# Moving a four-column transpose into an early matmul bank, and regrouping a chain of table transfers, in a two-layer fp32 decoder trunk

## The chip, the cores and the metric

One core of a Trainium2 chip runs the whole kernel in one launch. The metric is the device time of that core in microseconds (us). The kernel before was timed three times: median 1132.03 us, from 1131.14 to 1132.06 us. PE is the matmul engine (PEld its weight loads), ACT the scalar engine, DVE the vector engine, POOL the GpSimd engine; SP only issues transfers.

## The reference, cut to what matters

The input is one sequence of 512 tokens with 1024 features, all in fp32. Two layers are computed: attention and an MLP, then a short convolution mixer and a second MLP.

```python
for layer in range(2):
    if layer == 0:   # attention: 8 forgetting heads, 8 stick-breaking heads, width 64
        proj = rms_norm(h, attn_norm) @ attn_w_in
        q_fox = rms_norm(q[:, :8], fox_q_gain); k_fox = rms_norm(k[:, :8], fox_k_gain)
        q_sb  = rms_norm(q[:, 8:], sb_q_gain);  k_sb  = rms_norm(k[:, 8:], sb_k_gain)
        ...
        h = h + concat(o_fox, o_sb) @ attn_w_out
    else:            # short convolution
        b, c, u = split(rms_norm(h, conv_norm) @ conv_w_in)
        h = h + (b * causal_dwconv(c * u, conv_kernel)) @ conv_w_out
    u = causal_dwconv(rms_norm(h, ffn_norm[layer]) @ ffn_w_up[layer], ffn_conv[layer])
    h = h + (silu(u[:, :2816]) * u[:, 2816:]) @ ffn_w_down[layer]
```

Two things in it matter here. Each head's queries and keys are multiplied by a gain vector of 64 values (the head norms' factors). And the up-projection of each MLP multiplies 1024 features by a 1024 x 5632 matrix.

## The kernel before, in words

**Products.** Every fp32 operand is split into a high part (written by ACT, line 293 for weights) and a low part (DVE subtracts, line 294), and each product is three matmuls: high by high, high by low, low by high (lines 314 to 316, or 571 to 573 where tokens are the output rows). Weights come from DRAM through three `raw` buffers, issued by SP.

**The start.** The input `x_tok` arrives in four pieces. For each of eight blocks of 128 features, `take(f)` turns the block on PE (four transposes, line 857), ACT writes its high part (line 862) and DVE its low part (line 863). Between the blocks PE already runs the first head pair's key product, which is the first product of `queries_keys(0)`; the list `ORDER` says how many of its eight steps follow each block. Instructions of this stage are chained by `in_line`, which forces an instruction behind the last one that was chained on the same engine. After the eighth block come the rest of the key product, the whole query product, and then `values(0)`, the first value product: four token blocks of 24 matmuls (L571 to L573). PSUM is cut into banks by tag; tag `a` has two banks, `b` four and `c` two, each tag handed out in turn, and a bank must be read out before its next user may write.

The head gains (`heads_in`, four rows fetched by POOL at line 127) must be turned from rows into a column on every partition: one transpose (L188) into a `c` bank, a copy to `head_gains` (L189) and two scalings (L191). The kernel before asks for this step 4.0 us of counted PE work after the loads were issued (`after(HEADS, ...)`); it is then placed behind the query product. ACT's copy of each product out of its bank (L659) multiplies by `head_gains`, so it needs this step; and the first value product writes the `a` bank that the key product's copy frees. The sums of squares for the head norms (L608, eight small matmuls) and the transpose of the small parameters (L179) are placed behind it too.

**The up-projections.** Most of each MLP's up-projection, and the convolution's input projection, use Strassen-like forms on 2 x 2 blocks: seven block products (p1, p7, p3, p6, p2, q5, q4) instead of eight, class `Sevens`. A group of 256 output columns takes seven slots, one form each, 24 matmuls of about 0.12 us (L1055) a slot. The slot code also loads the next blocks (X, Y, W, Z on SP's queue, L1070, L1071, L1079) and adds blocks in flight (POOL, accumulating transfers, L1082). For the convolution the groups are 1 to 4, so there are 28 slots and three more behind them. Two X buffers exist; the group's p1 is made from X (ACT and DVE, L1003 and L1005), then Y gets X added (L1112), and only then may X be overwritten by an accumulating transfer, for q5.

**The tables.** For the MLPs the sums of blocks are made ahead in DRAM (`table_steps`): transfers of 256 rows x 768 columns, issued by POOL, alternately a copy (L104) and an accumulation (L101), each waiting for the one before it when it reads or changes the same table. The second MLP has 24 of them. The kernel takes steps from this generator by `sum_far(n)`: `FAR = 7, 1, 14` means seven after the attention, one at each of the convolution's slots 1, 8 and 15, and fourteen at slot 20. All POOL transfers go through one queue in program order.

Of the kernel before, what the change touches and what calls it, by code (L numbers as in the profile page):

```python
# [22 lines left out]
ALU = mybir.AluOpType  # L23
# [6 lines left out]
ND = D // P  # L30
DFF = 2816
NF = DFF // P
HD = 64
# [6 lines left out]
PRE = 12.0  # L40
SUM_STEP = 0.6
WARM = 34
HEADS, NORM0 = 4.0, 4.6
ORDER = (1, 0, 1, 1, 1, 1, 3)
SUMS, FLAT, ROWS = 3.0, 1.5, 8.0
NSUMS, NROWS, LATE = 4.0, 3.0, 7.0
FILL1, FILL2, BEFORE = 1.5, 3.3, 2.0
UNITS = (0, 1), (2,), (3,)
PLAIN = 2
FAR = 7, 1, 14  # L50
CHUNKS = (2, 3), (5, 3), (8, 3)
SHARE = 0.58

# [2 lines left out]
def trunk(  # L56
# [7 lines left out]
    act, dve, pe, pool = nc.scalar, nc.vector, nc.tensor, nc.gpsimd  # L64
# [12 lines left out]
    def bank(tag):  # L77
        n_ps[0] += 1
        return ps.tile([P, S], F32, tag=tag, name=f"ps{tag}{n_ps[0]}", bufs={"a": 2, "b": 4, "c": 2}[tag])
# [43 lines left out]
    heads_in = xin.tile([4, P], F32, tag="heads_in", name="heads_in")  # L123

    def load_heads():
        for i, g in enumerate((fox_q_gain, fox_k_gain, sb_q_gain, sb_k_gain)):
            nc.gpsimd.dma_start(heads_in[i:i + 1, :].rearrange("o (j d) -> o j d", j=2), g[:, None, :].to_broadcast([1, 2, HD]))
# [26 lines left out]
    ident = const.tile([P, P], F32, tag="ident", name="ident")  # L154
# [20 lines left out]
    head_gains = const.tile([P, 4], F32, tag="head_gains", name="head_gains")  # L175
# [7 lines left out]
            pe.transpose(t[:, i * 66:(i + 1) * 66], taps_in[:, i, :], ident[0:66, 0:66])  # L183
        dve.tensor_copy(taps, t[:, 0:4 * 66])

    def load_head_gains():
        t = bank("c")
        pe.transpose(t[:, 0:4], heads_in, ident[0:4, 0:4])  # L188
        dve.tensor_copy(head_gains, t[:, 0:4])  # L189
        for i in (0, 2):  # L190
            dve.tensor_scalar(head_gains[:, i:i + 1], head_gains[:, i:i + 1], HD ** -0.5, None, op0=ALU.mult)  # L191

    def gain_of(norm, f):
        return gains[:, norm + f:norm + f + 1]
# [9 lines left out]
    def behind(later, earlier):  # L204

        tc.add_manual_dep(
            later.ins, earlier.ins.name,
            mybir.DependencyInfo(mybir.DependencyClass.NoSync, mybir.DependencyReason.DATA), reason="order",
        )
# [11 lines left out]
    def after(us, fn):  # L221
        later.append((clock[0] + us, len(later), fn))
        later.sort(key=lambda e: e[0])
# [74 lines left out]
    def split_all(i):  # L298
        part, nk = halve.pop(i)
        return part(0, nk)  # L300

    def fetch(n):
        while len(ready) < min(len(wanted), at[0] + n):
            ready.append(load(len(ready)))
            split_all(len(ready) - 1)
# [28 lines left out]
    class Norm:  # L334
# [18 lines left out]
        def squares(self, f, src):  # L353
            if self.first:
                self.first = False
                act.activation(self.acc, src, AF.Square)
            else:
                sq = own.tile([P, S], F32, tag="sq", name=f"sq_{self.name}{f}")
                act.activation(sq, src, AF.Square)
                dve.tensor_tensor(self.acc, self.acc, sq, op=ALU.add)  # L360
# [473 lines left out]
    t = bank("c")  # L834
# [4 lines left out]
    t = bank("c")  # L839
# [8 lines left out]
    def in_line(engine, made):  # L848

        if engine in rows:  # L850
            behind(made, rows[engine])
        rows[engine] = made

    def take(f):
        t = taken[f] = bank("bbbbccbb"[f])
        for b in range(NB):
            in_line("pe", pe.transpose(t[:, b * P:(b + 1) * P], x_tok[:, b, f * P:(f + 1) * P], ident))

    def halves_of(f):
        t, g = taken[f], first_gains[:, f:f + 1]  # L860
        hi, lo = hs(f)
        in_line("act", act.activation(hi, t, AF.Copy, scale=g))
        in_line("dve", dve.scalar_tensor_tensor(lo, t, g, f32(hi), op0=ALU.mult, op1=ALU.subtract))

    def keep(f):
        t = taken.pop(f)
        if f % 2:
            in_line("act", act.activation(h[:, f, :], t, AF.Copy))
        else:
            in_line("dve", dve.tensor_copy(h[:, f, :], t))  # L870
# [8 lines left out]
    for i in range(1, 1 + AHEAD):  # L879
        ready.append(load(i))  # L880
    load_heads()
    after(HEADS, load_head_gains)
    qk0 = queries_keys(0)
    part, nk = halve.pop(0)

    def split_in_line(made):
        for engine, m in zip(("act", "dve"), made):
            in_line(engine, m)

    def first_products(n):  # L890
        for _ in range(n):
            for made in next(qk0):
                in_line("pe", made)
# [7 lines left out]
    for f in range(2, ND):  # L901
        take(f)
        halves_of(f)
        if f == 3:
            keep(0)
            keep(1)
        first_products(ORDER[f - 1])
    split_in_line(split_all(1))
    squares(0)
    squares(1)  # L910
# [59 lines left out]
    def sum_far(n):  # L970
        for _ in range(n):
            next(sums_far, None)

    sum_far(FAR[0])

# [328 lines left out]
    def conv_seven(norm, mp):  # L1304
# [126 lines left out]
        want_conv_out()  # L1431
        for s in range(28):
            up.slot(1 + s // 7, s % 7)
            if s in (1, 8, 15):
                sum_far(FAR[1])
            elif s == 20:
                sum_far(FAR[2])
            if s == 27:
                fetch(1)
        for s in (0, 2, 3):  # L1440
# [198 lines left out]
    with tc.tile_pool(name="mix", bufs=1, reuse_waits="tile") as mp:  # L1639
        ys = conv_seven(norm, mp)  # L1640
        norm = Norm("n3", 8)
        hs_open(2)

        def out_products(w, acc, ks):
            for k in ks:
                y_hi, y_lo = ys[k // 4]
                mm3(acc, (w[0][:, k, :], w[1][:, k, :]), (y_hi[:, k % 4, :], y_lo[:, k % 4, :]), k == 0, k == ND - 1)

        first_two = [(weights(AHEAD - o), bank("ab"[o])) for o in range(2)]
        for w, acc in first_two:  # L1650
            out_products(w, acc, range(6))
        for o, (w, acc) in enumerate(first_two):
            out_products(w, acc, (6, 7))
            if o:
                fetch(AHEAD)
            residual_out(o, acc, norm)
        for o in range(2, ND):
            w, acc = weights(), bank("ab"[o % 2])
            out_products(w, acc, range(ND))
            residual_out(o, acc, norm)  # L1660
        norm.finish()
# [29 lines left out]
```

## Time and profile before

| | |
|---|---|
| median of three runs | 1132.03 us |
| the profiled execution's own time | 1132.23 us |
| its span, first to last instruction | 1130.0 us |
| mean granted PE clock | 0.999 |
| bytes moved by transfers | 209.34 MB |

The profiled execution is 0.20 us above the median of the timed runs, and its time is 2.2 us above its span. In the profile, a row of the timeline reads: start in us, duration in us, engine, line, operation, output and inputs with their shapes, count, and in brackets the idle time before it on its engine and what ended that. SPq and POOL rows of transfers show the issue, not the data's flight; the time to landing is a view of its own. A wait row reads: engine, tile and line that waited, what it waited for, then total us, times, longest.

### The profile page before, as it was taken

Reading aid. Unit: us, or ns where it says so; the run is one execution under the profiler, and the core shown is the slowest. Engines: PE = TensorE matmul, PEld = TensorE weight load, DVE = VectorE, ACT = ScalarE, POOL = GpSimd, SP = SyncE. Lnnn points to the kernel's source line nnn. Section 1 sums busy time; section 2 is a strip of 40 time slices with the busy share of each in tenths; the row PEclk is TensorE's granted clock in tenths of the full one; section 3 lists DMA queues with packets and bytes.
Section 4 is the critical chain, followed back from the end, with each engine's and each line's share of the span. In section 5 each row is a group of like instructions: output and inputs, shape, how many; then the busy total and the mean of one; then the engine's idle time right before and its main releaser. Section 6 shows DMA issues by size and latency. Waiting matters only on the chain.

```text
span 1130.0 us, 19403 instructions
## 1 busy us (share of the span) xinstructions
PE 1116.2 (99%) x7691; PEld 1009.3 (89%) x7691; DVE 942.9 (83%) x1439; ACT 680.0 (60%) x1013; POOL 159.3 (14%) x191
## 2 busy tenths in 40 slices
PE   8999999999999999999999999999999999999998
PEld 7888787878899999999999889988889999998876
DVE  6787888887899787888979878875799888898886
ACT  7556676655466667676557345544456766677553
POOL 4011111111001110004300011111001110014300
PEclk9999999999999999999999999999999999999999
DMA  6678777777868777699953466899757766699961
GB/s 193 171 178 202 187 172 188 181 191 200 202 180 203 199 203 195 196 283 212 223 162 94 129 137 163 186 231 226 190 155 186 178 172 162 180 268 195 226 156 57
DMA packets 175690, 209.34 MB, mean 185 GB/s; under 512 B 7564, under 2 KB 140220, under 8 KB 175600
## 3 DMA queue, kind: packets, MB, share of 16 engines
q0 software_dynamic: 41024, 86.95, 38.8%
q1 hardware_dynamic: 134416, 121.09, 34.7%
q8 instruction: 60, 0.98, 0.4%
q14 instruction: 30, 0.25, 0.1%
q10 hardware_dynamic: 160, 0.07, 0.0%
HBM read 203.10 MB, written 49.28 MB: 223 GB/s over the span
## 4 chain that ended last, share of the span: by engine, by line
PE 87%; DVE 5%; DMA 3%; issue 2%; ACT 2%; DVEq 0%; ACTq 0%; POOLq 0%
PE psb L1055 25%; PE psb L1603 10%; PE psa L1055 10%; PE psa L1603 6%; PE psb L314 5%; PE psb L315 5%; PE psb L316 5%; PE psa L316 2%; PE psa L314 2%; PE psa L315 2%; DMA Xc<-in_conv_w_in 2%; PE psa L785 2%; PE psb L689 2%; DMA raw<-in_ffn_w_down 1%; DVE wlo L294 1%
## 5 line engine op out<-in xcount | busy, mean ns | idle before, releaser
L293 ACT ACTIVATE whi<-raw 128x1024 fp32r<-128x1024 f32 (+2 forms) x89 | 91.6, 1032 | 95.0 <-PE psb L315 29.7
L294 DVE TENSOR_TENSOR wlo<-raw,whi 128x1024 fp32r<-128x1024 f32 (+2 forms) x89 | 105.5, 1187 | 26.7 <-ACT whi L293 26.0
L1055 PE MATMUL psb<-p_lo,whi_p 128*128 128x256 f32 x432 | 121.6, 281 | 0.0
L1055 PE MATMUL psb<-p_hi,wlo_p 128*128 128x256 f32 x432 | 121.6, 281 | 0.0
L1055 PE MATMUL psb<-p_hi,whi_p 128*128 128x256 f32 x432 | 121.2, 281 | 0.0
L314 PE MATMUL psb<-hs_a,whi 128*128 128x512 f32 x224 | 92.2, 412 | 0.0
L316 PE MATMUL psb<-hs_a,wlo 128*128 128x512 f32 x224 | 88.7, 397 | 0.0
L1055 PEld LDWEIGHTS psb<-p_hi,whi_p 128*128 128x128 f32 x432 | 81.9, 190 | 0.0
L1055 PEld LDWEIGHTS psb<-p_lo,whi_p 128*128 128x128 f32 x432 | 81.3, 188 | 0.0
L1055 PEld LDWEIGHTS psb<-p_hi,wlo_p 128*128 128x128 f32 x432 | 81.2, 188 | 0.0
L1055 PE MATMUL psa<-p_hi,wlo_p 128*128 128x256 f32 x288 | 81.2, 282 | 0.0
L1055 PE MATMUL psb<-q_lo,whi_q 128*128 128x256 f32 x288 | 81.0, 281 | 0.0
L1055 PE MATMUL psa<-p_lo,whi_p 128*128 128x256 f32 x288 | 81.0, 281 | 0.0
L1055 PE MATMUL psb<-q_hi,wlo_q 128*128 128x256 f32 x288 | 81.0, 281 | 0.0
L1055 PE MATMUL psa<-p_hi,whi_p 128*128 128x256 f32 x288 | 80.8, 281 | 0.0
L1055 PE MATMUL psb<-q_hi,whi_q 128*128 128x256 f32 x288 | 80.8, 281 | 0.0
L1603 PE MATMUL psb<-act,whi 128*128 128x256 f32 x352 | 63.1, 282 | 0.1
L424 DVE SCALAR_TENSOR_TENSOR uv<-yv,taps,uv 128x511 f32<-128x511 f32 (+1 forms) x80 | 56.7, 747 | 0.0
L1603 PE MATMUL psb<-whi,act 128*128 128x512 f32 x176 | 56.3, 398 | 0.0
L424 DVE SCALAR_TENSOR_TENSOR ug<-yg,taps,ug 128x511 f32<-128x511 f32 (+1 forms) x80 | 55.7, 748 | 0.0
L1603 PEld LDWEIGHTS psb<-act,whi 128*128 128x128 f32 x352 | 54.2, 189 | 0.5 <-DVE act L1005 0.3
L1055 PEld LDWEIGHTS psa<-p_hi,whi_p 128*128 128x128 f32 x288 | 54.5, 189 | 0.1
(478 smaller groups left out, 3628.8 us busy)
## 6 DMA issues: line engine op xcount, KB each, us to landing
t<-in_ffn_w_up POOLq DMA_DIRECT2D x42, 768.0 KB, 8.2
t<-t POOLq DMA_DIRECT2D x18, 768.0 KB, 4.9
raw<-in_attn_w_in SPq DMA_DIRECT2D x24, 512.0 KB, 5.0
X<-in_ffn_w_up SPq DMA_DIRECT2D x18, 512.0 KB, 5.2
Y<-t SPq DMA_DIRECT2D x18, 512.0 KB, 6.1
three<-t SPq DMA_DIRECT2D x18, 512.0 KB, 3.7
W<-in_ffn_w_up SPq DMA_DIRECT2D x18, 512.0 KB, 4.0
X<-in_ffn_w_up POOLq DMA_DIRECT2D x18, 512.0 KB, 7.8
```

Source lines behind the costliest of these rows:

```text
L293: return (act.activation(hi[:, at_], raw[:, at_], AF.Copy), dve.tensor_tensor(lo[:, at_], raw[:, at_], f32(hi[:, at_]), op=ALU.subtract))
L294: dve.tensor_tensor(lo[:, at_], raw[:, at_], f32(hi[:, at_]), op=ALU.subtract))
L314: made = [pe.matmul(acc, w[0], rhs[0], start=first, stop=False), pe.matmul(acc, w[0], rhs[1], start=False, stop=False), pe.matmul(acc, w[1 ...
L315: pe.matmul(acc, w[0], rhs[1], start=False, stop=False),
L316: pe.matmul(acc, w[1], rhs[0], start=False, stop=last)]
L424: dve.scalar_tensor_tensor(dst[:, d:], src[:, 0:S - d], tap(j), dst[:, d:], op0=ALU.mult, op1=ALU.add)
L689: pe.matmul(ss[e][:, c:c + wide], ql[rows, b * P:n], kl[rows, 0:wide], start=first and b == bs[0], stop=last and b == bs[-1])
L785: pe.matmul(out_, w, t[:, first:first + step * (NB - k - 1) + 1:step, :], start=k == 0 and i == 0, stop=k == NB - 1 and i == 1)
L1055: pe.matmul(to, w[a][:, k, c], x[b][:, k, :], start=fresh and i + k + t == 0, stop=i == 1 and k == 3 and t == 2, skip_group_check=not fresh)
L1603: pe.matmul(to, l, r, start=begin and o + t == 0, stop=end and t == 2 and o == (0 if layer else 1), skip_group_check=not fresh)
```

## The change

Two edits. First, the head gains' step no longer waits on the count of PE work: it is written behind the seventh block's product steps (`f == ND - 2`), chained with `in_line` on PE and DVE, and its transpose goes into a bank of tag `a` that is taken just before the key product's. Second, the 24 table transfers of the second MLP are taken as eight after the attention and sixteen at the convolution's slot 20; slots 1, 8 and 15 take none.

```diff
-HEADS, NORM0 = 4.0, 4.6
+NORM0 = 4.6
...
-FAR = 7, 1, 14
+FAR = 8, 16
...
-    def load_head_gains():
-        t = bank("c")
-        pe.transpose(t[:, 0:4], heads_in, ident[0:4, 0:4])
-        dve.tensor_copy(head_gains, t[:, 0:4])
+    def load_head_gains(t):
+        in_line("pe", pe.transpose(t[:, 0:4], heads_in, ident[0:4, 0:4]))
+        in_line("dve", dve.tensor_copy(head_gains, t[:, 0:4]))
         for i in (0, 2):
-            dve.tensor_scalar(head_gains[:, i:i + 1], head_gains[:, i:i + 1], HD ** -0.5, None, op0=ALU.mult)
+            in_line("dve", dve.tensor_scalar(head_gains[:, i:i + 1], head_gains[:, i:i + 1], HD ** -0.5, None, op0=ALU.mult))
...
     load_heads()
-    after(HEADS, load_head_gains)
+    heads_bank = bank("a")
     qk0 = queries_keys(0)
...
         first_products(ORDER[f - 1])
+        if f == ND - 2:
+            load_head_gains(heads_bank)
     split_in_line(split_all(1))
...
-            if s in (1, 8, 15):
+            if s == 20:
                 sum_far(FAR[1])
-            elif s == 20:
-                sum_far(FAR[2])
```

Line numbers of the changed kernel stand one lower from the head gains on, and one higher from the seven-product code on (L314 is L313 there, L1082 is L1083).

PE in the kernel before, from the last steps of the query product (`psa_288`) to the first matmul of the value product (`psa_424`):

```order
L314 MATMUL psa_288<-hs_a_119,whi_169 128x512
L315 MATMUL psa_288<-hs_b_120,whi_169 128x512
L316 MATMUL psa_288<-hs_a_119,wlo_170 128x512
L188 MATMUL psc_268<-ident,heads_in 128x4
L608 MATMUL psc_459<-sq_284,head_ones 32x128 x4
L179 MATMUL psc_590<-ident,spare 128x48
L571 MATMUL psa_424<-whi_173,hs_a_119 128x264
```

PE in the changed kernel at the end of the first value block (`psa_424`) and the start of the second (`psa_452`), where the sums of squares (`head_ones`) now stand:

```order
L570 MATMUL psa_424<-whi_289,hs_a_119 128x264
L571 MATMUL psa_424<-wlo_290,hs_a_119 128x264
L572 MATMUL psa_424<-whi_289,hs_b_120 128x264
L607 MATMUL psc_459<-sq_284,head_ones 32x128 x4
L607 MATMUL psc_459<-sq_405,head_ones 32x128 x3
L570 MATMUL psa_452<-whi_173,hs_a_119 128x264
L571 MATMUL psa_452<-wlo_174,hs_a_119 128x264
L572 MATMUL psa_452<-whi_173,hs_a_119 128x264
```

Of the three pieces between the query product and the value product none is left there: the gains' transpose stands ahead of the eighth block's transposes, the sums of squares behind the first value block, and the small parameters' transpose behind the last.

DVE in the changed kernel, at the seventh and eighth blocks' low parts (`psb_246`, `psb_260`), where the gains' copy and scalings now stand, and the weight halves behind them:

```order
L862 SCALAR_TENSOR_TENSOR hs_b_120<-psc_236,first_gains,hs_a_119 128x512
L862 SCALAR_TENSOR_TENSOR hs_b_120<-psb_246,first_gains,hs_a_119 128x512
L188 COPY head_gains<-psa_182 128x4
L190 TENSOR_SCALAR head_gains<-head_gains 128x1 x2
L862 SCALAR_TENSOR_TENSOR hs_b_120<-psb_260,first_gains,hs_a_119 128x512
L293 TENSOR_TENSOR wlo_170<-raw_171,whi_169 128x1024
L293 TENSOR_TENSOR wlo_174<-raw_175,whi_173 128x1056
```

Before, the two block rows stand next to each other, and the copy stands behind three weight halves and two copies of blocks. On ACT, the key product's copy out of its bank (L659) moves from behind the fourth square of the input to between the second and the third of the three weight halves there.

POOL in the kernel before, in the convolution (X and Y of each group, and the table transfers `t` between them):

```order
L1082 DMA Xc_7649<-in_conv_w_in 128x4x256
L1082 DMA Yc_7762<-in_conv_w_in 128x4x256
L101 DMA t_3286<-in_ffn_w_up 256x768
L1082 DMA Xc_7761<-in_conv_w_in 128x4x256
L1082 DMA Yc_7957<-in_conv_w_in 128x4x256
L104 DMA t_3284<-in_ffn_w_up 256x768
L1082 DMA Xc_7956<-in_conv_w_in 128x4x256
L1082 DMA Yc_8191<-in_conv_w_in 128x4x256
L101 DMA t_3284<-in_ffn_w_up 256x768
L1082 DMA Xc_8190<-in_conv_w_in 128x4x256
L104 DMA t_3287<-t_3284 256x768
```

POOL in the changed kernel at the same place:

```order
L1083 DMA Xc_7650<-in_conv_w_in 128x4x256
L1083 DMA Yc_7763<-in_conv_w_in 128x4x256
L1083 DMA Xc_7762<-in_conv_w_in 128x4x256
L1083 DMA Yc_7957<-in_conv_w_in 128x4x256
L1083 DMA Xc_7956<-in_conv_w_in 128x4x256
L1083 DMA Yc_8190<-in_conv_w_in 128x4x256
L1083 DMA Xc_8189<-in_conv_w_in 128x4x256
L104 DMA t_3284<-in_ffn_w_up 256x768
L101 DMA t_3284<-in_ffn_w_up 256x768
L104 DMA t_3287<-t_3284 256x768
```

The three table transfers between the convolution's own are gone; the first of them stands in the attention's tail, the other two at the head of the batch behind the last X.

## The prediction

> **What bounds the kernel now.** The page comes first: who is busy.
>
> ```profile
> PE 1116.2 (99%) x7691; PEld 1009.3 (89%) x7691; DVE 942.9 (83%) x1439; ACT 680.0 (60%) x1013; POOL 159.3 (14%) x191
> ```
>
> PE is busy for all but 1130.0 - 1116.2 = 13.8 us of the span. The change takes no matmul away, so it can give only what PE waits. So the second view is PE's waits:
>
> ```profile
> PE psa L1055 <- ACT whi_p1c L1003: 1.8, 1, 1.8
> PE psc L641 <- DVE pt L765: 1.3, 1, 1.3
> PE psc L608 <- DVE pt L765: 1.1, 2, 0.7
> PE psa L1055 <- DVE wlo_p1c L1005: 1.0, 2, 0.8
> ...
> PE psb L1055 <- ACT Xsc L1107: 0.6, 1, 0.6
> PE psc L608 <- DVE head_gains L189: 0.5, 1, 0.5
> ```
>
> The two L765 rows belong to the attention, which the change leaves as it is. The others are the two places that it touches: the convolution (`c` at a name's end), with 1.8 + 1.0 + 0.6 = 3.4 us, and the head gains, with 0.5 us and a further 0.2 that the timeline below shows. That is the ceiling, 4.1 us; the third view, the timeline at each place, tells how much of it comes free.
>
> **Part one, the head gains.** PE's rows from the last query matmuls on; ACT's row for the key product's copy; and two of DVE, the eighth block's low part and the last reading of the first value block's bank:
>
> ```profile
> 21.76 0.40 PE L315 MATMUL psa<-hs_b,whi 128*128 128x512 f32 x1
> 21.99 0.40 PE L316 MATMUL psa<-hs_a,wlo 128*128 128x512 f32 x1
> 22.32 0.22 PE L188 MATMUL psc<-ident,heads_in 4*128 4x4 f32 x1
> 23.03 0.42 PE L608 MATMUL psc<-sq,head_ones 128*32 128x128 f32 x8 [0.49 <-DVE head_gains L189]
> 23.39 0.26 PE L179 MATMUL psc<-ident,spare 48*128 48x48 f32 x1
> 23.87 0.39 PE L571 MATMUL psa<-whi,hs_a 128*128 128x264 f32 x1 [0.22 <-ACT qk L659]
> ...
> 27.37 0.28 PE L572 MATMUL psa<-wlo,hs_a 128*128 128x264 f32 x1
> 27.49 0.28 PE L573 MATMUL psa<-whi,hs_a 128*128 128x264 f32 x1
> 27.70 0.43 PE L608 MATMUL psc<-sq,head_ones 128*32 128x128 f32 x8
> 28.05 0.40 PE L571 MATMUL psa<-whi,hs_a 128*128 128x264 f32 x1
> ```
> ```profile
> 23.13 0.69 ACT L659 ACTIVATE qk<-psa,head_gains 128x512 f32<-128x512 f32 x1
> ```
> ```profile
> 14.77 0.75 DVE L863 SCALAR_TENSOR_TENSOR hs_b<-psb,first_gains,hs_a 128x512 fp32r<-128x512 f32 x1 [0.38 <-ACT hs_a L862]
> ...
> 28.04 0.22 DVE L567 SCALAR_TENSOR_TENSOR gate<-psa,ncol_n,f_bias 128x8 f32<-128x8 f32 x1
> ```
>
> The query product's matmuls follow each other every 0.23 us, so the value product could begin at 22.22; it begins at 23.87, 1.65 us later, since its bank is the one that L659 frees, and ACT gets to L659 at 23.13 only. In the changed order L659 stands among ACT's weight halves, whole microseconds before the value product, and the gains are ready by 15. But the 1.65 us are not all waiting. Three pieces of work stand in them and only move: L188 (0.22), the first L608 group and L179 (0.26). What a group costs inside the stream is seen at 27.49: the next value matmul comes 0.56 later instead of 0.12, so 0.44. The gain is 1.65 - 0.22 - 0.44 - 0.26 = 0.73 us, and PE's idle brackets, 0.49 + 0.22 = 0.71, say the same.
>
> The moved step costs little where it goes. Its transpose delays the eighth block's transposes by about 0.2 us (the 0.22 just counted). DVE's copy and two scalings (three tiny rows) fall into the 0.38 us in which DVE waits for ACT before the eighth block; if they overrun it, PE, which waits for that block's low part, is late by the rest, at most 0.3. The new order splits the sums of squares into three runs where there were two; I take 0.1 off for one more switch. **Part one: 0.6 us, between 0.2 and 0.9.** Two covers must hold: the gains' rows must have landed (last issued at 4.56, longest flight 5.7, so 10.3, against a transpose shortly ahead of the DVE row at 14.77),
>
> ```profile
> 4.56 0.51 POOL L127 DMA_DIRECT2D heads_in<-in_sb_k_gain  x1
> ...
> DMA to landing us min/median/max: 5.0/5.6/5.7
> ```
>
> and the third value block needs the bank that DVE empties last at about 28.3 (L567); the first two blocks of 24 matmuls at 0.12 and 0.9 of sums from 22.4 on end at about 29. If the attention's own DVE waits (the L765 rows) grow by what PE arrives earlier, this part is lost whole: 0.
>
> **Part two, the table transfers.** The convolution's second group, from the transfers to PE's wait:
>
> ```profile
> 662.89 1.84 POOL L1082 DMA_DIRECT2D Yc<-in_conv_w_in  x1
> 663.64 2.06 POOL L101 DMA_DIRECT2D t<-in_ffn_w_up  x1
> ...
> 666.18 0.37 SPq L1070 DMA_DIRECT2D Xc<-in_conv_w_in  x1
> ...
> 677.71 1.06 ACT L1003 ACTIVATE whi_p1c<-Xc 128x1024 fp32r<-128x1024 f32 x1 [5.72 <-DMA Xc<-in_conv_w_in]
> 678.82 0.39 PE L1055 MATMUL psa<-p_hic,whi_p1c 128*128 128x256 f32 x1 [1.78 <-ACT whi_p1c L1003]
> 680.08 0.39 PE L1055 MATMUL psa<-p_hic,wlo_p1c 128*128 128x256 f32 x1 [0.76 <-DVE wlo_p1c L1005]
> ```
>
> The flights of Y's accumulation, of t, and of X's load, and the transfers' rate in steps of 1 us from 660 on:
>
> ```profile
> DMA to landing us min/median/max: 9.9/9.9/9.9
> ```
> ```profile
> DMA to landing us min/median/max: 13.8/13.8/13.8
> ```
> ```profile
> DMA to landing us min/median/max: 11.4/11.4/11.4
> ```
> ```profile
> GB/s 81 0 0 0 72 172 203 190 205 199 236 229 228 232 238 355 374 384 350 249 23 11 0 16 0 45 98 217 237 249 285 200 204 355 409 390 377 332 175 355
> ```
>
> Y lands at 672.8, t at 677.4, X at 677.6: X comes home with t. The rate row says why. From 664 to 675 it stands near 200 and moves 2204 kB; then it jumps to 350 to 384. POOL's queue held X's and Y's accumulations and t: 524 + 524 + 786 = 1834 kB. If that queue ran dry at the jump, SP's four loads (X, Z and the next X and Y, 524 kB each) had only 370 kB of the 2204: 34 kB/us from X's issue on at best, while POOL's queue took 1834 / 11 = 167 kB/us. Without t that queue is dry 786 / 167 = 4.7 us sooner, at 670.3. SP then has about 140 kB; X's other 384 kB take 1.0 us at 370 kB/us. Landing came 2.2 us after the last byte by this count (675.4 and 677.6), so X lands at about 673.5, 4.1 us sooner. PE needs it 1.2 us after landing for the first matmul, 2.5 us for the third, so at 674.7 and 676.0; PE comes free at about 677.0. The stall, 1.78 + 0.76 = 2.54 us, goes whole, with 1.3 us to spare.
>
> What is late next? The chain X, Y + X on DVE, the accumulation into X, q5 moves up by nearly 4 us, PE by 2.5. Two later waits hang on that chain:
>
> ```profile
> 700.56 0.38 PE L1055 MATMUL psa<-p_hic,wlo_p1c 128*128 128x256 f32 x1 [0.27 <-DVE wlo_p1c L1005]
> ...
> 715.39 0.39 PE L1055 MATMUL psb<-q_hic,whi_q5c 128*128 128x256 f32 x1 [0.60 <-ACT Xsc L1107]
> ```
>
> I take 0.27 and half of 0.60, since convolution rows on ACT and DVE stand in the second chain and follow PE. **Part two: 2.54 + 0.27 + 0.30 = 3.1 us, between 0 and 3.4.**
>
> The three transfers turn up elsewhere. One follows the attention's seven, beside the first MLP's first loads. Y is the one wanted soonest after its issue:
>
> ```profile
> 307.78 0.37 SPq L1071 DMA_DIRECT2D Y<-t  x1
> ```
> ```profile
> 321.83 1.04 ACT L1003 ACTIVATE whi_p<-Y 128x1024 fp32r<-128x1024 f32 x1
> ```
>
> Those 14 us cover even a flight as long as X's 11.4 above, so I cost it at nothing. Two go to the batch's head:
>
> ```profile
> 753.24 0.59 POOL L104 DMA_DIRECT2D t<-t  x1 [8.65 <-DMA t<-in_ffn_w_up]
> ...
> 808.11 0.88 POOL L101 DMA_DIRECT2D t<-in_ffn_w_up  x1 [4.71 <-DMA t<-t]
> ...
> 831.84 1.33 POOL L1082 DMA_DIRECT2D X<-in_ffn_w_up  x1 [22.85 <-DVE wlo_p L1005]
> ```
> ```profile
> 842.22 1.05 ACT L1003 ACTIVATE whi_q<-X 128x1024 fp32r<-128x1024 f32 x1
> ```
>
> A link takes 9.5 us (an issue of 0.88 and the 8.65 waited at 753.24), two 19. The last transfer is issued at 808.1 + 19 - 3.7 = 823.5 instead of 808.1; the next POOL transfer, X of the second MLP, is wanted at 831.8 - 3.7 = 828.1. It is still in front, with 4.6 us left. I cost it at nothing; without that cover PE would pay one for one, since X is used 842.2 - 831.8 = 10.4 us after its issue and POOL's Y above flew 9.9.
>
> **The sum.** From the profiled execution, 1132.23: 0.6 + 3.1 = 3.7 less, 1128.5. Its time lies 0.20 above the median of the timed runs, inside what such runs differ by, so I leave it.
>
> **A page against it.** The Trainium skill, page "DMA: Bandwidth & Descriptors", section "Queues, rings and completion order", says that each transfer engine serves the queues that have work in turn, a packet at a time. By that rule with packets of like size, X's load would have had half of the 200 kB/us of the rate row, and been through about 5 us after its issue, t or no t. The trace does not agree: the load took 11.4 us. A packet of t may be larger than one of X's load; no row here shows it.
>
> **The rivals.**
> 1. *The queues share evenly, and X is late through something else* (its slowest share of the transfer, or Y's accumulation). For it: no row names the transfer that an engine works on. Against it: two landings 0.2 us apart, and the rate's jump. Then part two gives nothing: 1132.2 - 0.6 = 1131.6. Chance 0.16.
> 2. *t costs X only part*: X lands 1 to 2.5 us sooner, the third matmul still waits, and the later waits stay. Part two gives about 1.5: 1130.1. Chance 0.11.
> 3. *The attention absorbs part one*, its DVE waits taking up what PE gains: 3.1 alone, 1129.1. Chance 0.13.
> 4. *Slower: the batch of sixteen holds the second MLP's X.* POOL's Y and t above landed in the order of issue. If the two links cost 30 us instead of 19, in the stage where the output weights are loaded too, the last table transfer is issued at 808.1 + 30 - 3.7 = 834.4, and X behind it instead of at 828.1; with 0.5 us to spare PE loses 5.8 us against 3.7 gained, and the time is 1134.3. From 28 us for the two on, the loss is larger than the gain. Against it: 9.5 us a link was read in that very stage. Chance 0.05.
>
> **Numbers.** The forecast, 1128.5, has a chance of 0.55. A measurement of this kernel can tell about 0.2%, 2.3 us, from no change, so faster means below 1129.8. Forecast and rival 3 are faster: 0.68. Rivals 1 and 2 are within: 0.27. Rival 4 is slower: 0.05. The lower end takes both ceilings (0.9 + 3.4) from the fastest run, 1131.1: 1126.8. The upper end takes in rivals 2, 3 and most of 1: 1131.7.
>
> **What would show it.** In the changed profile: the value product begins about 1.2 us earlier than 23.87, with no bracket for `head_gains` or L659; PE's wait for `whi_p1c` is gone and X's second load flies 6 to 9 us; the rate jumps to 350 about 4 us after X's issue; the waits of 0.27 and 0.60 shrink; the last table transfer is issued near 823 and the second MLP has no PE wait. The prediction is wrong if X still flies 11 us with no t beside it, if the attention's L765 waits grow by 0.6, or if a PE wait stands behind 800.

## The result, and the profile after

| | before | changed | ratio, 95% interval |
|---|---|---|---|
| median of seven runs each | 1131.58 us | 1127.65 us | 0.9967, 0.9956 to 0.9978 |
| the profiled execution's own time | 1132.23 us | 1127.62 us | |
| its span | 1130.0 us | 1125.3 us | |

The change takes 3.9 us off the median, 0.22 to 0.44% by the interval. The forecast was 1128.5, in 1126.8 to 1131.7.

The page of the changed kernel, its row of busy times: PE does the same 7691 matmuls and waits for 1125.3 - 1115.6 = 9.7 us of the span, 4.1 less than before.

```profile
PE 1115.6 (99%) x7691; PEld 1009.8 (90%) x7691; DVE 943.4 (84%) x1439; ACT 679.9 (60%) x1013; POOL 158.6 (14%) x191
```

PE's waits in the changed kernel (total us, times, longest): the rows of the convolution and of the head gains are gone, and the two of the attention (L764, L765 before) are as they were. The row of L313 (L314 before) differs between executions, whatever the kernel: 0.9 us before, 1.2 here, 0.9 in both repeats of the changed kernel.

```profile
PE psc L640 <- DVE pt L764: 1.3, 1, 1.3
PE psa L313 <- ACT whi L292: 1.2, 1, 1.2
PE psc L607 <- DVE pt L764: 1.1, 2, 0.7
PE psc L835 <- DVE blank L116: 1.0, 1, 1.0
PE psa L784 <- DVE o L791: 0.5, 1, 0.5
```

**The start.** Three views of the changed kernel, PE, DVE and ACT. The transpose of the gains (L187) now stands at 13.14, the value product's first matmul (L570) follows the query product's last without a gap, and ACT's L658 is done at 19.7.

```profile
13.14 0.22 PE L187 MATMUL psa<-ident,heads_in 4*128 4x4 f32 x1
...
21.94 0.39 PE L315 MATMUL psa<-hs_a,wlo 128*128 128x512 f32 x1
22.17 0.28 PE L570 MATMUL psa<-whi,hs_a 128*128 128x264 f32 x1
```
```profile
13.94 0.15 DVE L188 COPY head_gains<-psa 128x4 f32<-128x4 f32 x1
14.12 0.21 DVE L190 TENSOR_SCALAR head_gains<-head_gains 128x1 f32<-128x1 f32 x2
14.71 0.75 DVE L862 SCALAR_TENSOR_TENSOR hs_b<-psb,first_gains,hs_a 128x512 fp32r<-128x512 f32 x1 [0.37 <-ACT hs_a L861]
```
```profile
19.06 0.68 ACT L658 ACTIVATE qk<-psa,head_gains 128x512 f32<-128x512 f32 x1
```

**The convolution's second group.** SP's issue of X, ACT's first work on it, and PE's first matmul from it, which carries no bracket now. The load flew 6.9 us, and so landed at 672.8:

```profile
665.90 0.37 SPq L1071 DMA_DIRECT2D Xc<-in_conv_w_in  x1
```
```profile
672.89 1.06 ACT L1004 ACTIVATE whi_p1c<-Xc 128x1024 fp32r<-128x1024 f32 x1 [1.18 <-DMA Xc<-in_conv_w_in]
```
```profile
676.60 0.28 PE L1056 MATMUL psa<-p_hic,whi_p1c 128*128 128x256 f32 x1
```

The transfers' rate, in steps of 1 us from 660 on, has its jump to 340 and more at 670, where it was at 675:

```profile
GB/s 8 0 0 10 97 193 197 194 189 222 342 380 371 347 348 253 19 0 0 0 36 109 186 236 253 278 193 200 285 342 266 253 3 65 316 160 0 0 0 0
```

**Where the 4.7 us of span come from.** The first row of the convolution's input projection and of the second MLP's up-projection, before and changed:

```profile
659.59 0.28 PE L1055 MATMUL psa<-p_hic,whi_p1c 128*128 128x256 f32 x1
...
834.89 0.28 PE L1055 MATMUL psa<-p_hi,whi_p 128*128 128x256 f32 x1
```
```profile
659.31 0.28 PE L1056 MATMUL psa<-p_hic,whi_p1c 128*128 128x256 f32 x1
...
830.62 0.28 PE L1056 MATMUL psa<-p_hi,whi_p 128*128 128x256 f32 x1
```

0.28 us are gained ahead of the convolution, 3.99 in its stage (175.30 against 171.31), and 0.4 behind it. These are two single executions: in two more profiles of the changed kernel the stage took 172.32 and 171.97, so that a difference between two profiles below 1 us says little here. The head gains gave more than 0.28, but lost it again. PE's first matmul of the first MLP's up-projection and of its down-projection, before and changed:

```profile
324.14 0.28 PE L1055 MATMUL psa<-p_hi,whi_p 128*128 128x256 f32 x1
...
500.31 0.39 PE L1603 MATMUL psa<-act,whi 128*128 128x256 f32 x2
```
```profile
323.29 0.28 PE L1056 MATMUL psa<-p_hi,whi_p 128*128 128x256 f32 x1
...
500.10 0.40 PE L1602 MATMUL psa<-act,whi 128*128 128x256 f32 x2
```

0.85 us ahead at the one, 0.21 at the other: 176.17 us of matmuls have become 176.81, with no wait and a granted clock of 1.00 in both.

### The profile page after: what moved, and what is told of

It reads as the page before. It is cut to its first block, busy times and chain, and to the rows that moved or that the text cites. A ratio compares the mean times of both kernels' runs of the same rounds, so it can differ in the third digit from the quotient of the medians.

```text
span 1125.3 us, 19407 instructions
## 1 busy us (share of the span) xinstructions
PE 1115.6 (99%) x7691; PEld 1009.8 (90%) x7691; DVE 943.4 (84%) x1439; ACT 679.9 (60%) x1013; POOL 158.6 (14%) x191
## 4 chain that ended last, share of the span: by engine, by line
PE 90%; DVE 4%; issue 2%; DMA 2%; ACT 1%; SPq 0%; DVEq 0%; ACTq 0%; POOLq 0%
PE psb L1056 25%; PE psb L1602 11%; PE psa L1056 10%; PE psa L1602 8%; PE psb L313 5%; PE psb L315 5%; PE psb L314 5%; PE psa L315 3%; PE psa L313 3%; PE psa L314 3%; PE psa L784 2%; PE psb L688 2%; DMA Xc<-in_conv_w_in 2%; PE psb L570 1%; PE psc L315 1%
## 5 line engine op out<-in xcount | busy, mean ns | idle before, releaser
L313 PE MATMUL psb<-hs_a,whi 128*128 128x512 f32 x224 | 92.2, 412 | 0.0
L1056 PEld LDWEIGHTS psb<-q_hi,whi_q 128*128 128x128 f32 x288 | 54.6, 189 | 0.0
```

Of the source, the lines that this page charges most:

```text
L313: made = [pe.matmul(acc, w[0], rhs[0], start=first, stop=False), pe.matmul(acc, w[0], rhs[1], start=False, stop=False), pe.matmul(acc, w[1 ...
L1056: pe.matmul(to, w[a][:, k, c], x[b][:, k, :], start=fresh and i + k + t == 0, stop=i == 1 and k == 3 and t == 2, skip_group_check=not fresh)
```

## The experiments

The theory on trial is the forecast's: GpSimd's queue serves t, the table transfer in slot 1, ahead of or beside SP's load of X, and X comes home with t. Its rivals: the gain is the head gains'; the transfers in slots 8 and 15 matter as much; and, on how t costs, that the queues share by bytes rather than by packets. All medians stand beside the kernel before on the same chip. The times in the table's middle columns are read from one profile of each kernel, the last column from medians.

| kernel | t in the convolution's slots | SP's issue of X to ACT's work on it, us | PE's stall in group two, us | first matmul of the convolution to that of the second MLP, us | against before, us |
|---|---|---|---|---|---|
| before | 1, 8, 15 | 11.5 | 2.54 | 175.30 | |
| head gains alone | 1, 8, 15 | 10.9 | 1.93 | 175.13 | -0.4 |
| slot 1 kept alone | 1 | 11.7 | 2.72 | 176.60 | -0.5 |
| two in slot 1 | 1 (two) | 13.4 | 4.07 | 177.81 | +1.2 |
| slot 1 in three pieces | 1 | 9.6 | 0.76 | 173.93 | -1.3 |
| slot 1 free | 8, 15 | 7.5 | 0 | 172.55 | -3.4 |
| tables alone | none | 7.5 | 0 | 171.30 | -4.0 |
| changed | none | 7.0 | 0 | 171.31 | -3.9 |

### The two parts apart

Tables alone (against the kernel before; the slots' line becomes `if s == 20: sum_far(FAR[1])`):

```diff
-FAR = 7, 1, 14
+FAR = 8, 16
-            if s in (1, 8, 15):
+            if s == 20:
                 sum_far(FAR[1])
-            elif s == 20:
-                sum_far(FAR[2])
```

> The table part alone (eight after the attention, sixteen at slot 20); the head gains stay as before. My theory: the transfer t at slot 1 holds back the load of X for the second group, and the two later waits hang on the same chain. Then the three waits in the convolution go, the second group's p1 starts 3.1 us earlier against the slots, the third group gains 0.5 twice, and the time is about 4.1 us below that of before; the wait of 0.5 and 0.2 us at the head gains stays. Rival: the late X has another cause and the whole gain comes from the order at the start: then the time is that of before.

Measured: 1128.08 against 1132.11, ratio 0.9963 (0.995 to 0.9975), as the theory had it: the three waits of the convolution are gone from its profile.

Head gains alone (against the changed kernel, the reverse of these lines):

```diff
-FAR = 8, 16
+FAR = 7, 1, 14
-            if s == 20:
+            if s in (1, 8, 15):
                 sum_far(FAR[1])
+            elif s == 20:
+                sum_far(FAR[2])
```

> The head gains' part alone; the table transfers stay as before. My theory: the value product starts 1.7 us earlier, 0.75 us of it are left once the sums of squares and the small parameters' transpose are done, and nothing downstream takes them back: 0.6 to 0.9 us below before, with the three convolution waits unchanged (1.8, 1.0, 0.6). Rival: the attention's waits for DVE grow by what the start gives: no change.

Measured: 1131.73 against 1132.11, ratio 0.9998 (0.999 to 1.0007). The stall in the convolution is there, as these brackets of its PE rows show:

```profile
678.04 0.38 PE L1056 MATMUL psa<-p_hic,whi_p1c 128*128 128x256 f32 x1 [1.17 <-ACT whi_p1c L1004]
...
679.30 0.39 PE L1056 MATMUL psa<-p_hic,wlo_p1c 128*128 128x256 f32 x1 [0.76 <-DVE wlo_p1c L1006]
```

What follows: the time that the change saves is that of the tables. The head gains alone can't be told from no change, though its theory's start holds (the value product begins at 22.13) and the attention's waits are 1.3 and 1.1 us as before, against the rival.

### Which of the three transfers

Slot 1 free (against the kernel before):

```diff
-FAR = 7, 1, 14
+FAR = 8, 1, 14
-            if s in (1, 8, 15):
+            if s in (8, 15):
```

> Before, with the one transfer of slot 1 moved behind the attention (eight, then one each at slots 8 and 15, fourteen at slot 20). My theory: slot 1's is the only one that costs, since the later waits hang on the chain that its X starts: X's load flies about 7 us instead of 11.4, all three waits go, about 4 us below before. Rival: the transfers at slots 8 and 15 make the third group's two waits by themselves: those two stay, about 3 us below before.

Measured: 1128.7 against 1132.11, ratio 0.9967 (0.9955 to 0.998). No stall in group two. The theory had all three waits go; two later ones of PE, both in group three, are left, as the rival had it:

```profile
698.22 0.39 PE L1055 MATMUL psa<-p_hic,wlo_p1c 128*128 128x256 f32 x1 [0.41 <-DVE wlo_p1c L1005]
...
713.12 0.39 PE L1055 MATMUL psb<-q_hic,whi_q5c 128*128 128x256 f32 x1 [0.68 <-ACT Xsc L1107]
```

Slot 1 kept alone (against the kernel before):

```diff
-FAR = 7, 1, 14
+FAR = 7, 1, 16
-            if s in (1, 8, 15):
+            if s == 1:
```

> Before, with the transfers of slots 8 and 15 moved into the batch (seven after the attention, one at slot 1, sixteen at slot 20). My theory: nothing is gained; X flies about 11 us, the second group's p1 waits as before (3.1 us by the starts), and the third group's waits of 0.3 and 0.6 stay: within 0.3 us of before. Rival (the later waits come from slots 8 and 15): about 1 us below before, the first wait alone staying.

Measured: 1131.58 against 1132.11, ratio 0.9998 (0.9989 to 1.0007). The stall is there; the two later waits, which the theory kept, are not in this profile. What follows: slot 1's transfer is the cost. For the other two the medians leave 0.5 to 0.6 us (1131.58 against 1132.11 here, 1128.08 with the tables alone against 1128.7 with slot 1 free), which can't be told from nothing.

### How t holds X up

Two in slot 1 (against the kernel before, slots 8 and 15 empty as in the last run): a second transfer right behind the first.

```diff
-FAR = 7, 1, 14
+FAR = 7, 2, 15
-            if s in (1, 8, 15):
+            if s == 1:
```

> Two table transfers at slot 1 instead of one, none at slots 8 and 15, fifteen at slot 20. My theory (POOL's queue is emptied almost alone, and SP's load waits for it): X lands 4 to 5 us later than with one, PE's wait for it grows by the same 4 to 5 us, and the time is about 4.5 us above before. Rival (the two queues share evenly, X's lateness has another cause): X flies 11 us as before and the time stays that of before.

Measured: 1133.56 against 1132.36, ratio 1.0011 (0.9999 to 1.0022): as a time it can't be told from the kernel before, and neither the theory's 4.5 us nor the rival's unchanged X came about. X takes 1.7 us longer from its issue than with one t (13.4 against 11.7), not the 4 to 5 longer that a second 786 kB at the 167 kB/us of the forecast's count would make it.

Slot 1 in three pieces (against the kernel before, with 16 in the batch and slot 1 kept alone): the same bytes, in three transfers of 256 columns each, so that a row of it is 1 kB instead of 3.

```diff
-                        pin(nc.gpsimd.dma_start(to, src[rows, :], accum_op=ALU.add))
+                        cut = 256 if layer and g == 2 and rows.start and step == 3 else m * 256
+                        for c in range(0, m * 256, cut):
+                            pin(nc.gpsimd.dma_start(to[:, c:c + cut], src[rows, c:c + cut], accum_op=ALU.add))
...
-            if s in (1, 8, 15):
+            if s == 1:
```

> One table transfer at slot 1, but cut into three transfers of 256 columns, so that each row moved is 1 kB like the rows of X, and not 3 kB; the same bytes. If the share of a queue goes by rows (packets) and not by time, X's load gets more of the engines beside t and lands 1.5 to 3 us sooner than 11 us after its issue, and PE's wait shrinks by the same. If POOL's queue simply goes first, or if accumulation is what is slow, X lands as late as with one transfer or later (11 us or more), and PE's wait is the 3.1 us of before or more.

Measured: 1131.01 against 1132.36, ratio 0.999 (0.9979 to 1.0002). As a time it can't be told from the kernel before. In the profile X takes 2.1 us less from its issue than with the same transfer in one piece, and of PE's stall only the second bracket (0.76) is left.

These rows settle how. They are the profile's transfer queues in one microsecond, with packets, MB, and their share of 16 engines' time: q0 is GpSimd's, q1 is SP's. The kernel before, 671 to 672 us; two in slot 1, 675 to 676; three pieces, 672 to 673; and the changed kernel, 671 to 672:

```profile
q0 software_dynamic: 60, 0.17, 87.9%
q1 hardware_dynamic: 58, 0.06, 21.8%
```
```profile
q0 software_dynamic: 61, 0.32, 81.4%
q1 hardware_dynamic: 65, 0.06, 19.1%
```
```profile
q0 software_dynamic: 122, 0.11, 71.3%
q1 hardware_dynamic: 120, 0.12, 44.1%
```
```profile
q1 hardware_dynamic: 383, 0.38, 107.0%
q0 software_dynamic: 4, 0.00, 1.9%
```

The packets of the two queues are nearly equal in number, 60 and 58, 61 and 65, 122 and 120, whatever they hold: 2.8 kB against 1.0 in the kernel before, 5.2 against 1.0 with the second t (why its packets are larger than its rows of 3 kB no view shows), 0.9 against 1.0 in three pieces. The neighbouring microseconds, with both queues at work, say the same: 58 and 58, 57 and 56 from 672 to 674 in the kernel before. X gets 0.06 MB in that microsecond beside a packet of 2.8 kB, 0.12 beside one of 1 kB, and 0.38 alone. The Trainium skill, page "DMA: Bandwidth & Descriptors", section "Queues, rings and completion order", says that an engine serves its queues in turn a packet at a time. The trace agrees, in the packets that the profile counts.

That fits two in slot 1 as well. X is 512 packets of 1 kB. Counted along SP's queue in steps of 1 us, 373 had gone by 675 in the kernel before, when t was through, and the other 139 took 0.4 us. With a second t 433 had gone by 676, and the rest went on at about 70 in a microsecond: the 512th packet is some 1.6 us later, 677.0 against 675.4, which is how late X was: ACT starts on it at 679.28 against 677.71. By this count a transfer in the other queue can hold X up by no more of its packets than X itself still has to move.

### The batch's side: how much room is there?

Eighteen in the batch (against the changed kernel):

```diff
-FAR = 8, 16
+FAR = 6, 18
```

> The changed kernel with six transfers after the attention and eighteen at slot 20, so that the batch ends two transfers later. My theory of the batch's margin: in the changed kernel the last transfer is issued at 824.6 and the second MLP's X at 827.6; two more transfers (about 5 and 9 us) put the last at about 838 to 840, X behind it 11 us late, and PE waits 7 to 11 us for q5 of that group: 1135 to 1139. Rival: the margin is wider, since X is not used for 10 us after its issue: at most 3 us of wait, below 1131.

Measured: 1129.32 against 1132.36, ratio 0.9998 (0.9964 to 1.0031; it is not the quotient of the two medians, which five runs so far apart move); its five runs lie between 1127.41 and 1136.63. Inconclusive as a time. GpSimd's rows of the changed kernel and of this one, the last table transfer and the second MLP's X:

```profile
824.62 0.87 POOL L101 DMA_DIRECT2D t<-in_ffn_w_up  x1 [7.28 <-DMA t<-t]
827.55 1.33 POOL L1083 DMA_DIRECT2D X<-in_ffn_w_up  x1 [2.07 <-DVE wlo_p L1006]
```
```profile
826.57 0.88 POOL L101 DMA_DIRECT2D t<-in_ffn_w_up  x1 [6.73 <-DMA t<-t]
827.69 1.33 POOL L1083 DMA_DIRECT2D X<-in_ffn_w_up  x1 [0.24 <-DVE wlo_p L1006]
```

In the profiled execution, the fastest of the five, the batch ended at 826.57 and not at the theory's 838 to 840, and X was still issued when it was wanted, with 0.24 us to spare. Whether the long runs are those in which the batch was later was not seen, since only one execution has a trace.

Twenty in the batch (against the changed kernel):

```diff
-FAR = 8, 16
+FAR = 4, 20
```

> The changed kernel with the tables' transfers split four and twenty instead of eight and sixteen. In the changed kernel the batch's sixteen ran from 720.4 to 824.6 us, 6.9 us from one issue to the next, and the eighteen of the run before from 720.5 to 826.6, 6.2 us; twenty would have their last issue at 838 to 852. The second MLP's load of X on the same queue is wanted at 827.6. Theory (the queue is in order, so a late batch holds that load, and PE waits for it one for one behind at most a microsecond of spare): X issued behind the last table transfer at 838 or later, a wait of PE of 9 us or more in the second MLP's up-projection, and 1137 to 1151. Rival (the second MLP's loads reach PE by another way, or the spare is large): no wait of PE there, and 1127 to 1129. The loads of the convolution stay as in the changed kernel under both: X's first piece on ScalarE 7 us after the issue.

Measured: 1144.97 against 1132.39, ratio 1.012 (1.0093 to 1.0148). GpSimd's rows, and PE's first matmul from that X:

```profile
845.24 0.88 POOL L101 DMA_DIRECT2D t<-in_ffn_w_up  x1 [4.64 <-DMA t<-t]
845.80 1.67 POOL L1083 DMA_DIRECT2D X<-in_ffn_w_up  x1
```
```profile
857.54 0.58 PE L1056 MATMUL psb<-q_hi,whi_q 128*128 128x256 f32 x1 [12.79 <-ACT Xs L1108]
```

The theory holds: a late batch holds X, and PE pays. Of the 15.2 us of span over the changed kernel beside it (1142.2 against 1127.0) 12.8 are this wait and 1.4 a later start of the convolution (660.96 against 659.53). The windows of this kernel (us, PE busy, granted clock, transfers' share, GB/s) show PE at half clock behind the wait, where its matmuls take longer:

```profile
840.00:856.00 16.00, 4.74 (x41) 0.74 0.91 179
856.00:860.00 4.00, 2.46 (x11) 0.50 0.03 5
860.00:864.00 4.00, 4.00 (x31) 0.85 0.74 228
```

Ten and fourteen (against the changed kernel):

```diff
-FAR = 8, 16
+FAR = 10, 14
```

> The changed kernel with the split at ten and fourteen: two more transfers behind the attention, and the batch two shorter. Theory (the place behind the attention costs PE nothing, and neither does a shorter batch): 1127 to 1128.5, no wait of PE in the first MLP, the batch's last transfer issued before 820. Rival (transfers behind the attention are shared packet by packet with the first MLP's loads, whose first use comes 14 us after the issue, and three more than in the kernel before are too many): a wait of PE in the first MLP between 320 and 345 us, 1129 or more. It also says whether the first MLP's up-projection takes 176.8 us, as in the changed kernel and in the run with the head gains alone, or 176.2, as in the six others.

Measured: 1128.61 against 1132.39, ratio 0.9964 (0.9951 to 0.9977). The time is the theory's within 0.1 us, and the batch's last transfer is issued at 804.26; but ten behind the attention are not quite free, as the rival had it: in the profile PE waits in the first MLP, half a microsecond.

```profile
335.52 0.39 PE L1056 MATMUL psb<-q_hi,whi_q 128*128 128x256 f32 x1 [0.50 <-ACT Xs L1108]
```

### What repeats, and the slower first up-projection

The changed kernel, unedited, twice more, the second time beside the last kernel of this section:

> The changed kernel once more, nothing edited. If the slower first up-projection (176.8 us from its first matmul to the down-projection's first, against 176.2 in the kernel before, with no wait) belongs to this program, it is there again; if it is a matter of the execution, the profile shows 176.2 and the span is some 0.6 us shorter. The time under both: 1127 to 1128.5.

Measured: 1128.92 against 1132.39, ratio 0.9968 (0.9957 to 0.9979).

> The changed kernel unedited, on the same chip as the run with six, two and sixteen, for the difference between the two. 1127 to 1129, and 176.8 us for the first up-projection as in both profiles of it so far.

Measured: 1128.53 against 1132.08, ratio 0.9966 (0.9954 to 0.9979). The gain is 3.9, 3.5 and 3.6 us in the three comparisons. Both profiles have the 176.8 us of the first up-projection again. Both also have a later wait of the convolution that the first profile of the changed kernel lacks; in the first of them it is these rows:

```profile
697.47 0.38 PE L1056 MATMUL psa<-p_hic,wlo_p1c 128*128 128x256 f32 x1 [0.30 <-DVE wlo_p1c L1006]
...
712.35 0.38 PE L1056 MATMUL psb<-q_hic,whi_q5c 128*128 128x256 f32 x1 [0.66 <-ACT Xsc L1108]
```

Six, two and sixteen (against the changed kernel), a try for a better version: fewer behind the attention, and two in a stretch of GpSimd's queue that looked empty.

```diff
-FAR = 8, 16
+FAR = 6, 2, 16
...
-                sum_far(FAR[1])
+                sum_far(FAR[2])
...
         norm = mlp(0, norm, mp)
+        sum_far(FAR[1])
```

> The changed kernel with the tables' transfers in three places: six behind the attention, two behind the first MLP, where GpSimd's queue has nothing from 597.6 to 661.9 us in the profile of the changed kernel, and sixteen in the batch. Two questions. The first up-projection took 176.8 us with the head gains moved and seven, eight or ten transfers behind the attention (177.6 with ten), and 176.2 with the gains moved and six or four, and in all kernels with the old gains. Theory (the number behind the attention decides it, together with the gains): 176.2, and the convolution starts some 0.6 us earlier than in the changed kernel. Rival (those were chance): 176.8. And the two transfers in the new place: free, since GpSimd's queue is empty; no wait of PE from 600 to 680, X's first piece on ScalarE 7 to 8 us after X's issue. Time by the theory 0.5 us below the changed kernel beside it, so some 1127 to 1128, which is less than these medians differ by and is to be read from the profile.

Measured: 1130.35 against 1132.08, ratio 0.9987 (0.9978 to 0.9996), 1.8 us above the changed kernel on the same chip. The up-projection takes 176.16 us, as the theory said; but the place was wrong. GpSimd issues the two at 561 and 573, ahead of the 597 that the expectation counted on, beside the last loads of the down-projection, and PE waits there once, while ACT waits 3.17 us for the last raw weights (1.89 in the changed kernel):

```profile
561.63 1.10 POOL L104 DMA_DIRECT2D t<-t  x1
...
573.40 0.91 POOL L101 DMA_DIRECT2D t<-in_ffn_w_up  x1 [10.67 <-DMA t<-t]
```
```profile
573.51 1.06 ACT L292 ACTIVATE whi<-raw 128x1024 fp32r<-128x1024 f32 x1 [3.17 <-DMA raw<-in_ffn_w_down]
```
```profile
576.49 0.39 PE L1602 MATMUL psa<-act,whi 128*128 128x256 f32 x1 [0.96 <-DVE act L1008]
```

That is 0.96 of the 1.8 us; the rest is not traced. So no version that beats the changed kernel was found. On the up-projection: all kernels with the old gains (six profiles, with seven or eight transfers behind the attention) took 176.16 or 176.17 us; with the gains moved, those with four or six transfers took 176.16 (three profiles), and those with seven or eight took 176.80 to 176.83 (four profiles, three of them of the same program). Ten took 177.58, the wait above included. So it goes with the program, not with the execution. Why the matmuls follow each other 0.36% more slowly there, and not in the second MLP, stays open.

## Why the prediction was right, step by step

**The ceiling** held: of the 4.1 us that PE waited at the two places, all went in the first profile.

**Part one, 0.6 us (0.2 to 0.9).** The mechanism was right: the value product follows without a gap, 1.70 us earlier where the forecast looked for about 1.2, since the moved transpose delayed nothing (the query product's last matmul stands at 21.94, and at 21.99 before). The pieces that only moved took the larger part back, to 0.73 at the attention's first logits (51.97 before, 51.24 changed). DVE's steps fell into its wait for ACT, as costed. The attention absorbed nothing: its two waits are 1.3 and 1.1 us as before. At the first MLP the seven profiles with the gains moved, that with twenty in the batch left out for its 2.0 us wait at L313, start at 323.3 to 323.8 us, the six without at 323.7 to 324.6: 0.8 us apart in the mean. What failed is what the step left out: with seven or eight transfers behind the attention the first up-projection gives back 0.64. By the convolution's first matmul 0.28 was left, and the kernel with the gains alone was 0.4 below the kernel before, with an interval around no change. So the 0.6 of the sum isn't confirmed as time.

**Part two, 3.1 us (0 to 3.4).** X on time, the stall gone whole: right. X was forecast to land at 673.5, 4.1 us sooner; it landed at 672.8, ACT starts on it at 672.89, 4.8 sooner, and PE came at 676.60 with X's halves ready, so the rest is spare. The stage gave 3.99, 2.98 and 3.33 us in the three profiles of the changed kernel, against 175.30 in the one profile of the kernel before. The term of the stall measures, slot 1 free against before, 175.30 - 172.55 = 2.75 against the 2.54 of the brackets, one profile of each. The later terms, 0.27 and 0.30, rested on a chain that moves up. They can't be confirmed: those waits are gone in the first profile and in that of the tables alone, but the second of them, at 0.63 to 0.84 us, stands in the six other profiles with no table transfer in the slots, both repeats among them, and it is missing with slot 1 kept alone and with two in it. So t is not what makes it, and it comes and goes between executions of one program.

**The sum**, 3.7, against 3.9, 3.5 and 3.6 measured, came out in part by luck. The tables alone gave 4.0, and none of the changed kernel's medians is below theirs by more than 0.5 (1127.65, 1128.92 and 1128.53 against 1128.08): part one's 0.6 did not arrive as time, and part two gave more than its 3.1.

**The count of bytes** in that step was the wrong picture with the right end. It gave SP's loads 370 kB up to the jump, and they had 373 packets of 1 kB, but not at an even 34 kB/us from X's issue on. They had two packets until 669, as X's began to move 2 to 3 us after its issue, and 60 kB/us from 670 to 674 while t ran. The jump is at the end of t's packets, as the step said. Where the two pictures part, at two transfers in slot 1, the one of packets was right.

**The page against it.** The forecast found that the trace did not agree with the packet rule, since X took 11.4 us and not 5. That was the weakest sentence of it: the queues' rows of the kernel before, quoted above, show nearly equal numbers of packets, and t's are 2.8 times as large. The possibility was named, and the rows that decide it were in the trace.

**Rival 1, X late through something else**, is refuted by slot 1 free. **Rival 2, only part of the stall**, is what cutting t in three gives, not what moving it does. **Rival 3** is refuted by the attention's waits. **Rival 4, slower through the batch**, did not come about with sixteen: the last table transfer was issued at 824.62 (forecast 823.5) and X at 827.55 (828.1). The mechanism is real, and the room small: eighteen left 0.24 us in one execution, twenty cost 16 us against sixteen. There X was issued some 16 us after it was wanted (845.80; in the changed kernel it is issued 3.1 us ahead of the second MLP's first matmul, which here stands at 832.76, so 829.7 by estimate), and PE waited 12.8: the cover was some 3 us, not the rival's 0.5. The two added transfers made the batch, from its first issue to its last, 104.3 us long (720.4 to 824.6) instead of 83.4 (724.7 to 808.1): 20.9 for the forecast's 19; 103.8 and 99.5 in the repeats.

**The eighth transfer behind the attention** was costed at nothing, and no wait came of it; two more brought one of 0.5 us. The slower first up-projection is there with seven as well, once the head gains are moved, so the eighth alone is not its cause.

## What to carry to other kernels

When a load comes home late, look at the transfer queues' packets in a window around it, not at the bytes alone: the two queues here shared by packets, so a bulk transfer with long rows beside an urgent load with short ones takes its larger share, and cutting its rows, or issuing it elsewhere, gives the load its time back. Bulk work that is moved out of an urgent stage needs a place with slack on its queue at both ends: here the same queue's next load was 3 us behind the batch's end, and four more transfers in it cost four times what the change gained. A wait in one profile below a microsecond, far from the edit, should not be counted as part of a change's gain until a second profile shows it.

## What was not expected of the hardware

**A stall costs more than its length in some executions.** The windows of the kernel with slot 1 kept alone: behind a stall of 1.99 and 0.73 us, hardly longer than the 1.78 and 0.76 before, PE's granted clock is at half, and its matmuls follow each other every 0.21 us instead of 0.12 until 686.3.

```profile
676.00:680.00 4.00, 1.69 (x12) 0.94 1.02 342
680.00:684.00 4.00, 3.59 (x17) 0.50 0.03 10
684.00:688.00 4.00, 4.00 (x27) 0.71 0.55 71
```

In the profile of the kernel before the same stretch has 1.00 throughout, so the forecast could not see this, and with the gains alone 1.93 us of stall were followed by 0.62 for 4 us. The Trainium skill, page "TensorE: Matmul & The Clock Gate", section "Part 1: The HAM clock gate (the "warmup" mystery)", tells of a clock that is halved after an idle window of about 3.4 us, where the windows run freely. That nearly the same stall is followed by half clock in one execution and not in the next fits windows that run freely; a stall below 3.4 us, broken by two matmuls, was enough here. Of 67 timed runs of the kernel before 37 have a mean clock of 0.998 or less, of 21 of the changed kernel one; but the 37 are only 0.6 us longer in the median than the other 30 (1132.57 against 1131.93), so this is a small part of the 3.5 to 3.9 us.
